# Layer B's attention: TensorE kept in source order, each group in four steps between the k products of the projection tiles

## The chip, the cores and the metric

The kernel runs on one core of a Trainium2 chip. The metric is the device time of one execution in microseconds (us); lower is better. One profiled execution gives the trace.

## The reference, cut to what matters

The model is a decoder trunk of two layers, run for 1024 prompt tokens and 8 decode samples together (1032 columns). The change touches only the second layer, "layer B", and there only the attention. In short:

```python
proj = rms_norm(h) @ w_in_b                      # 768 query columns and 256 memory-query columns
q = rope(proj[..., :768]); cq = proj[..., 768:]
tok_out = swa_attend(q, k, v, sinks)             # 12 heads of 64, window 128, 4 key/value heads, a sink per head
x_out = mem_attend(cq, mem_k, mem_v)             # 4 heads of 64 over 256 memory tokens
h = h + rms_norm(concat(tok_out, x_out) @ w_out) # then the MLP
```

All is float32. Each float32 product is made of three matmuls on rounded halves (high and low part of both operands), so a projection of 1024 inputs has 8 products k = 0 to 7 of three matmuls each.

## The kernel before, in words

The token columns stand in three chunks of 344. A **projection chunk** is one output tile of 128 features over one chunk: `dense_chunk` calls `dense_mm` (L298), which issues 8 products (24 matmuls, L287 to L289) into one PSUM bank of tag `dn`, which has two, and an evacuation by ScalarE follows (L1519).

The **attention** works in 32 groups. A group is one head over 512 tokens: groups 0 to 7 are memory attention, 8 to 31 sliding window. A group has these stages:

- `s1`: 8 score matmuls (L517, L518 or L1602, L1603) into two PSUM banks of tag `ax`, which has four; VectorE reads the maxima (for the window groups it also adds the mask into the tile `Pm`, L1606), ScalarE takes the exponentials (L525 or L1613). The tile `Pm` has tag `p` with four buffers.
- `norm`: VectorE makes the reciprocal of the sums, GpSimd multiplies `Pm` by it in two halves (L431).
- `s2`: 8 transposes of `Pm` on TensorE (L442) into two `ax` banks; each half is rounded by ScalarE and its rest taken by VectorE (`split`, L224) into tiles of tag `t`, which has two buffers, so one group's.
- `s3`: the value matmuls (L460; 4 for a memory group, 10 for a window group) into a bank of tag `ac`, which has two.
- `s4`: ScalarE copies one half (L468), VectorE adds the other, SyncE stores the result to `mixs`.

`run_groups` (L496) calls these one step per group: step i issues `s1` of group i+2, `norm` of i+1, `s3` of i-1, `s2` of i, then the other work that the list `fill` holds for this step, then `s4` of i-1. `fill` holds the 18 chunks of the six query tiles at steps -2, -1, 0, then 4 to 6, 8 to 10, 12 to 14, 16 to 18 and 19 to 21; the three chunks of the second key tile at 7, 11 and 15; rotary embedding and splitting of the queries and keys (`rope`, whose half rotation goes through a transfer, L1526); attention of the samples (`mem_sample` at 8 to 18, `swa_sample` at 26 to 30); and from step 23 on parts of the output projection: 8 chunks `early` of 5 products, 4 chunks `rest` of 3, one `full` of 8. Steps 1 to 3 and 22 hold no projection chunk.

The order of this source is not the order on the engines. When the kernel is built, a scheduler that simulates the engines chooses each engine's order: source order is only the priority, and an instruction whose operands the simulation takes as not ready is overtaken by a later one that is. The order so chosen is fixed in the program. The wrapper `InOrder` (L41) can tie an instruction behind the one traced before it on its engine; before the change it is used for VectorE in part of the MLP alone:

```python
return tc.keep_in_program_order(r) if ordered[0] else r
```

After `run_groups` come the rest of the output projection (`full`, `rest`), the norms and the MLP.

Of the kernel before, what the change touches and what calls it, by code (L numbers as in the profile page):

```python
# [10 lines left out]
F32R = mybir.dt.float32r  # L11
# [5 lines left out]
P = 128  # L17
D = 1024
KT = D // P
# [15 lines left out]
def trunk_kernel(ctx, tc, xT, memT, wia, wib, wkk, wkv, wmk, wo, wu, wd, cmk, cmv, sth, ssk, ssv,  # L35
                 gains, sinkb, sinkc, cosd, sind, identd, lvmd, swmd,
                 yT, mko, mvo, hpo, kpo, vpo, hso, kso, vso):
    nc = tc.nc
    ordered = [False]

    class InOrder:  # L41


        def __init__(self, eng):
            self.eng = eng

        def __getattr__(self, name):
            f = getattr(self.eng, name)

            def call(*args, **kw):  # L50
                r = f(*args, **kw)  # L51
                return tc.keep_in_program_order(r) if ordered[0] else r
            return call

    V, A, T, G, S = nc.vector, nc.scalar, nc.tensor, nc.gpsimd, nc.sync
    V = InOrder(V)
    uid = [0]

    def nm(s):
# [13 lines left out]
    def slot(tag, shape=(P, N), dt=F32):  # L73
        return spool.tile(list(shape), dt, tag=tag, name=nm(tag), bufs=BUFS[tag])
# [211 lines left out]
    def mm3(ps, wh, wl, xh, xl, first, last, more=False):  # L286
        T.matmul(ps, wh, xl, start=first, stop=False, skip_group_check=more)  # L287
        T.matmul(ps, wl, xh, start=False, stop=False, skip_group_check=more)  # L288
        T.matmul(ps, wh, xh, start=False, stop=last, skip_group_check=more)  # L289

    wide, turn_ = [False], [0]

    def dense_bank():
# [4 lines left out]
    def dense_mm(w, c, ks=range(KT), bank=None):  # L298
        ps = (psum(bank) if bank else dense_bank())[:, :CH]
        ks = list(ks)  # L300
        for i, k in enumerate(ks):
            mm3(ps, w[0][:, k * P:(k + 1) * P], w[1][:, k * P:(k + 1) * P], X[:, k, 0, cs(c)], X[:, k, 1, cs(c)],
                i == 0, i == len(ks) - 1)
        return ps

    def dense_chunk(w, c, evac, ks=range(KT)):
# [98 lines left out]
    class Group:  # L405
# [6 lines left out]

        def s1(self):
            self.Pm, self.den = slot("p", (P, 4, 256)), slot("sm", (P, 4))
            self.sink = self.s1f(self.Pm, self.den)

        def norm(self):
            if self.sink is not None:
# [12 lines left out]
                    tt(G, o, o,  # L431
                       self.den[:, j].unsqueeze(2).to_broadcast([P, o.shape[1], o.shape[2]]), ALU.mult)

        def s2(self):
            self.PT = hi, lo = [slot("t", (P, 2 * 512), F32R) for _ in range(2)]
            for hf in range(2):
                ps = psum("ax")
                blocks = [(2 * hf + i // 2, i % 2) if self.window else (i, hf) for i in range(4)]
                i0 = 1 if self.first and hf == 0 else 0
                for i, (j, kb) in enumerate(blocks):  # L440
                    if i >= i0:
                        T.transpose(ps[:, i * P:(i + 1) * P], self.Pm[:, j, kb * P:(kb + 1) * P], ident)  # L442
                sl = slice(hf * 512 + i0 * P, hf * 512 + 512)
                split(ps[:, i0 * P:], hi[:, sl], lo[:, sl], V)

        def s3(self):
            av = self.av = psum("ac")
# [24 lines left out]
    AHEAD = 2  # L472

    def group_steps(gs):

        n = len(gs)

        def do(stage, i):
            if 0 <= i < n:
                getattr(gs[i], stage)()  # L480

        def step(i):
            do("s1", i + AHEAD)
            do("norm", i + 1)
            do("s3", i - 1)
            do("s2", i)
            yield
            do("s4", i - 1)

        out = []  # L490
        for i in range(-AHEAD, n + 1):
            g = step(i)
            out += [lambda g=g: next(g, None)] * 2
        return out

    def run_groups(gs, fill):  # L496
        for i, f in enumerate(group_steps(gs)):
            f()
            if i % 2 == 0:
                for f in fill.get(i // 2 - AHEAD, ()):  # L500
                    f()

    def mem_groups(p, qs, k2, mv, r8):
        gs = []
        for hf in range(2):
            for e in range(2):
                h = 2 * p + e

                def s1(Pm, den, hf=hf, e=e, h=h):
                    mx = slot("sm", (P, 4))  # L510
                    for qq in range(2):
                        ps = psum("ax")
                        for u in range(2):
                            i = hf * 4 + qq * 2 + u
                            o = ps[:, u * 256:(u + 1) * 256]
                            ql = qs[e][:, i * P:(i + 1) * P]
                            T.matmul(o, ql, k2[0][:, h], start=True, stop=False)  # L517
                            T.matmul(o, ql, k2[1][:, h], start=False, stop=True)  # L518
                        m2 = mx[:, 2 * qq:2 * qq + 2]
                        V.reduce_max(m2, ps.rearrange("p (u k) -> p u k", u=2), axis=AX.X)  # L520
                        i0 = hf * 4 + qq * 2
                        V.scalar_tensor_tensor(m2, m2, -1.0, r8[:, i0:i0 + 2], op0=ALU.mult, op1=ALU.mult)
                        for u in range(2):
                            j = 2 * qq + u
                            A.activation(Pm[:, j], ps[:, u * 256:(u + 1) * 256], AF.Exp, bias=mx[:, j:j + 1],  # L525
                                         scale=r8[:, i0 + u:i0 + u + 1], accum_out=den[:, j:j + 1])
                gs.append(Group(e, s1, lambda kb, h=h: mv[:, kb, h * P:(h + 1) * P],
                                lambda ro, src, hf=hf: S.dma_start(mixs[6 + p][ro, hf * 512:(hf + 1) * 512], src)))
        return gs
# [519 lines left out]
    def mlp(l, hsrc, hdst, nxt, Yp):  # L1049
# [394 lines left out]
            weight_load(n)  # L1444
        for n in range(SPLIT, len(ust)):
            hidden_load(n)
        ordered[0] = True
        for n in range(SPLIT):
            hidden_split(n)
            weight_split(n)  # L1450
# [2 lines left out]
        for n, (p, cc, (g, m)) in enumerate(units):  # L1453
            if n + LOAD < len(units):
                weight_load(n + LOAD)
            if n + STAGE < len(units):
                hidden_load(n + STAGE)
            if n + SPLIT < len(units):
                hidden_split(n + SPLIT)
            if n + SPLIT < len(units):  # L1460
                weight_split(n + SPLIT)
            w = split_at.pop(n)
            for c in cc:
                if g == 0:
# [12 lines left out]
            if p == 4 and g == 1:  # L1477
                squares(0, 0, m, cc[0], G)
            if (g, m) == (3, 3):
                if p == 3:  # L1480
                    bg.append(lambda: None)
                    norm(1, 1)
                    norm(1, 0)
                if p == 4:
                    if cc[0] == 0:
                        bg.extend([lambda: None] * 2)
                    norm(0, cc[0])
            elif p in (2, 4):
                tick(1.6 if p == 2 else 1)
            if n + SPLIT >= half:  # L1490
                ordered[0] = False


    def swa_values(wv, vt, kvn, c, r1):
# [87 lines left out]
    def swa_groups(p, qs, ks, vt, swm):  # L1582
        j = p // 3
        gs = []
        for hf in range(2):
            for e in range(2):
# [3 lines left out]
                def s1(Pm, den, hf=hf, e=e, hh=hh):  # L1590
                    kh, kl = ks[e]
                    mx, es = slot("sm", (P, 4)), slot("sm", (P, 4))
                    for qq in range(2):
                        bank = psum("ax")
                        todo = []
                        for jj in (2 * qq, 2 * qq + 1):
# [18 lines left out]
                    return es  # L1615

                def vsrc(t, hf=hf, kvh=kvh):
                    blk = 4 * hf + t - 1
# [272 lines left out]
    def at(i, f, *args):  # L1891
        fill.setdefault(i, []).append(lambda: f(*args))
    load, put, weight, early, rest, full, norm, YB = out_b(hs[1], hs[2])
    parts = ((21, 0, (6, 7, 0)), (22, 0, (1, 2)), (23, 1, (6, 7, 0)), (24, 1, (1, 2)), (25, 0, (3,)), (25, 1, (3,)),
             (27, 2, (6, 7, 0)), (28, 2, (1, 2)), (29, 2, (3,)))
# [13 lines left out]
        at(i, weight, m, (tag, tag))  # L1909
    for p in range(6):  # L1910
        for c in range(NCH):
            at(start[p] + c - (0 if p else AHEAD), q[p][c])
    for c in range(NCH):
        at((7, 11, 15)[c], k1_step, c)
    for i, f in enumerate(mem_sample(1, cqs)):
        at(8 + i, f)
    for i, fs in zip((26, 27, 28, 28, 29, 30, 30), swa_sample(qss, knew)):
        for f in fs:
            at(i, f)
    for i, f, m, c in ((23, early, 0, 0), (24, early, 1, 0), (25, early, 2, 0), (26, early, 0, 1), (27, early, 1, 1), (28, early, 2, 1), (29, early, 3, 0), (30, early, 3, 1), (29, rest, 0, 0), (30, rest, 1, 0), (30, rest, 2, 0), (31, rest, 3, 0), (32, full, 4, 0)):  # L1920
        at(i, f, m, c)
    for i, *h in parts:
        at(i, load, *h)
    run_groups(groups, fill)
    weight(6, ("c", "c"))
    weight(7, ("r", "r"))
    for c in range(NCH):
# [109 lines left out]
```

## Time and profile before

| | |
|---|---|
| three runs | 2542.4, 2543.6, 2545.7 us; median 2543.6 |
| the profiled execution's own time | 2528.8 us |
| its span, first to last instruction | 2526.9 us |
| TensorE busy | 2337.0 us, 92% |
| VectorE, ScalarE, GpSimd busy | 67%, 44%, 56% |
| mean granted TensorE clock | 0.971 of 2.4 GHz |

The profiled execution was 14.8 us shorter than the median run; its span and what lies around it make its own time. Times in the trace count from the first instruction. The attention that the change touches lies between 1436 and 1733 us, in slices 23 to 28 of the 40 of the profile's page.

### The profile page before, as it was taken

The numbers are of one execution on the slowest core, as the hardware profiler recorded it, in microseconds if no ns is written. First come the engines' busy times: TensorE is split into PE (matmuls) and PEld (weight loads), VectorE is DVE, ScalarE is ACT, GpSimd is POOL, SyncE is SP. The second block draws the span as 40 slices with busy tenths as digits, with TensorE's granted clock in tenths as the row PEclk, the third lists the DMA queues.
The fourth block names the chain that finished last, engine by engine and source line by source line (L and its number), as shares of the span: only waits on it lengthen the run. The fifth ranks groups of instructions, "written<-read, shape, count | busy, mean of one in ns | idle before, by whom it ended". The sixth has DMA issues, their size and how long they took to land. (4 is left out here: it accounts for less than half of the span.)

```text
span 2526.9 us, 45370 instructions
## 1 busy us (share of the span) xinstructions
PE 2337.0 (92%) x17055; PEld 2258.4 (89%) x17055; DVE 1693.0 (67%) x2813; ACT 1105.7 (44%) x2457; POOL 1423.9 (56%) x1130
## 2 busy tenths in 40 slices
PE   7998999989899999999999998888999999999997
PEld 6887989989799989999998897777999899999996
DVE  7778677775766665677667367765576665667847
ACT  6573434444433232444354364664443333344424
POOL 4546454453676564657775344544576556557846
PEclk9999999999999999999999998999999999999998
DMA  4335555432345555755663333333335545855482
GB/s 160 134 109 177 164 179 168 161 95 84 113 138 165 167 183 175 246 162 149 197 214 112 106 105 97 108 111 132 120 113 167 171 156 171 277 148 152 127 279 74
DMA packets 231735, 383.00 MB, mean 152 GB/s; under 512 B 27914, under 2 KB 118602, under 8 KB 231500
## 3 DMA queue, kind: packets, MB, share of 16 engines
q1 hardware_dynamic: 154332, 253.80, 30.1%
q10 hardware_dynamic: 77184, 126.31, 17.1%
q8 instruction: 134, 2.20, 0.4%
q14 instruction: 85, 0.70, 0.1%
HBM read 253.27 MB, written 123.56 MB: 149 GB/s over the span
## 5 line engine op out<-in xcount | busy, mean ns | idle before, releaser
L287 PE MATMUL dn<-X,ws 128*128 128x344 f32 (+2 forms) x1136 | 374.0, 330 | 30.8 <-DVE X L51 17.7
L288 PE MATMUL dn<-X,ws 128*128 128x344 f32 (+2 forms) x1136 | 369.0, 325 | 0.0
L289 PE MATMUL dn<-X,ws 128*128 128x344 f32 (+2 forms) x1136 | 368.2, 324 | 0.0
L98 POOL TENSOR_TENSOR ws<-wr,ws 128x512 fp32r<-128x512 f32 (+1 forms) x118 | 222.4, 1887 | 172.3 <-ACT ws L225 161.9
L287 PEld LDWEIGHTS dn<-X,ws 128*128 128x128 f32 x1136 | 219.2, 193 | 41.7 <-DVE X L51 20.2
L51 DVE TENSOR_TENSOR X<-ws,X 128x516 fp32r<-128x516 f32 x160 | 179.6, 1127 | 107.0 <-ACT X L225 106.4
L288 PEld LDWEIGHTS dn<-X,ws 128*128 128x128 f32 x1136 | 219.6, 193 | 1.9 <-issue 0.8
L289 PEld LDWEIGHTS dn<-X,ws 128*128 128x128 f32 x1136 | 219.4, 193 | 1.2 <-issue 0.4
L288 PE MATMUL ax<-X 128*128 128x258 f32 x736 | 209.5, 285 | 2.2 <-POOL X L98 2.2
L287 PE MATMUL ax<-X 128*128 128x258 f32 x736 | 207.8, 284 | 3.0 <-ACT X L225 3.0
L289 PE MATMUL ax<-X 128*128 128x258 f32 x736 | 209.1, 285 | 0.0
L225 ACT CAST ws<-wr 128x1024 fp32r<-128x1024 f32 (+1 forms) x138 | 116.1, 843 | 148.1 <-DMA wfd<-ws 35.5
L98 POOL TENSOR_TENSOR p<-p,sm 128x512 f32<-128x512 f32 (+2 forms) x92 | 87.5, 974 | 127.3 <-DVE sm L51 66.7
L225 ACT CAST X<-ws 128x516 fp32r<-128x516 f32 (+1 forms) x192 | 110.1, 621 | 101.1 <-PE ax L289 48.3
L287 PE MATMUL ax<-X,ws 128*128 128x344 f32 (+2 forms) x472 | 148.0, 315 | 3.1 <-DVE X L51 2.7
L289 PE MATMUL ax<-X,ws 128*128 128x344 f32 (+2 forms) x472 | 145.8, 309 | 0.0
L288 PE MATMUL ax<-X,ws 128*128 128x344 f32 (+2 forms) x472 | 145.5, 308 | 0.0
L287 PE MATMUL ac<-X 128*128 128x258 f32 x496 | 140.2, 284 | 4.6 <-ACT k L1231 3.8
L288 PEld LDWEIGHTS ax<-X 128*128 128x128 f32 x736 | 140.8, 191 | 2.6 <-POOL X L98 2.6
L287 PEld LDWEIGHTS ax<-X 128*128 128x128 f32 x736 | 140.0, 191 | 3.4 <-ACT X L225 3.4
L289 PE MATMUL ac<-X 128*128 128x258 f32 x496 | 140.5, 284 | 0.0
L289 PEld LDWEIGHTS ax<-X 128*128 128x128 f32 x736 | 140.5, 191 | 0.0
(650 smaller groups left out, 8198.3 us busy)
## 6 DMA issues: line engine op xcount, KB each, us to landing
ws<-u ACTq DMA_DIRECT2D x160, 258.0 KB, 2.8
u<-k SPq DMA_DIRECT2D x104, 258.0 KB, 3.9
wr<-wu ACTq DMA_DIRECT2D x104, 256.0 KB, 3.1
wfd<-ws SPq DMA_DIRECT2D x20, 1024.0 KB, 5.0
X<-u21s SPq DMA_DIRECT2D x32, 516.0 KB, 6.3
ct<-u ACTq DMA_DIRECT2D x112, 129.0 KB, 2.7
u<-k SPq DMA_DIRECT2D x104, 129.0 KB, 1.8
u21s<-mv SPq DMA_DIRECT2D x26, 516.0 KB, 3.8
```

The source lines that it names most:

```text
L51: r = f(*args, **kw)
L98: return eng.tensor_tensor(out, a, b, op=op)
L225: A.copy(hi, src)
L287: T.matmul(ps, wh, xl, start=first, stop=False, skip_group_check=more)
L288: T.matmul(ps, wl, xh, start=False, stop=False, skip_group_check=more)
L289: T.matmul(ps, wh, xh, start=False, stop=last, skip_group_check=more)
```

## The change

The wrapper now also covers TensorE, and during `run_groups` every TensorE instruction is tied behind the one traced before it. The stages of a group are cut: `s1` and `s2` each into two halves of one PSUM bank. Step i is now four parts in another order: (1) `s3` of i-1 and the first half of `s2` of i; (2) its second half and `s4` of i-1; (3) the first half of `s1` of i+2 and `norm` of i+1; (4) the second half of `s1` of i+2. Part 1 comes first; the others are called from inside `dense_mm`, between two products k, when a quarter, half and three quarters of the products of that step are out. In a step without projection chunks the four parts follow each other. `fill` has the same entries at the same steps, with the count of their products added. No arithmetic changes.

```diff
-    V, A, T, G, S = nc.vector, nc.scalar, nc.tensor, nc.gpsimd, nc.sync
-    V = InOrder(V)
+    A, G, S = nc.scalar, nc.gpsimd, nc.sync
+    V, T = InOrder(nc.vector, "V"), InOrder(nc.tensor, "T")
...
+    between = []
+
+    def breath():
+
+        if between:
+            between[0]()
...
                 i == 0, i == len(ks) - 1)
+            if i < len(ks) - 1:
+                breath()
         return ps
...
-            self.sink = self.s1f(self.Pm, self.den)
+            self.half = self.s1f(self.Pm, self.den)
+            next(self.half)
+
+        def s1b(self):
+            self.sink = next(self.half)
...
         def step(i):
-            do("s1", i + AHEAD)
-            do("norm", i + 1)
-            do("s3", i - 1)
-            do("s2", i)
+            do(i - 1, "s3")
+            do(i, "s2")
             yield
-            do("s4", i - 1)
+            do(i, "s2b")
+            do(i - 1, "s4")
+            yield
+            do(i + AHEAD, "s1")
+            do(i + 1, "norm")
+            yield
+            do(i + AHEAD, "s1b")
...
     def run_groups(gs, fill):
...
+        steps = group_steps(gs)
+        for i in range(len(steps) // 4):
+            todo, fs = steps[4 * i:4 * i + 4], fill.get(i - AHEAD, ())
+            total, done = sum(k for _, k in fs), [0]
+
+            def due():
+                done[0] += 1
+                while todo and 4 * done[0] >= total * (4 - len(todo)):
+                    todo.pop(0)()
+            between[:] = [due] if total else []
+            todo.pop(0)()
+            for f, k in fs:
+                f()
+                if k:
+                    due()
+            between.clear()
+            while todo:
+                todo.pop(0)()
...
+    ordered.update("T")
     run_groups(groups, fill)
+    ordered.clear()
```

## Rows read from the trace of the kernel before

**Rows 1.** The page: the engines' busy time, and TensorE's granted clock in 40 slices.

```profile
PE 2337.0 (92%) x17055; PEld 2258.4 (89%) x17055; DVE 1693.0 (67%) x2813; ACT 1105.7 (44%) x2457; POOL 1423.9 (56%) x1130
PEclk9999999999999999999999998999999999999998
```

**Rows 2.** Busy us (count) by stretch for PE, PEld, DVE, ACT, POOL; clock; DMA.

```profile
1436.20:1453.50 17.30, 12.51 (x77) 12.05 (x76) 9.94 (x21) 11.23 (x25) 9.41 (x8) 0.84 0.37 125
1453.50:1523.50 70.00, 65.82 (x411) 60.68 (x410) 49.14 (x99) 41.24 (x114) 31.94 (x27) 0.97 0.35 97
1523.50:1657.20 133.70, 118.91 (x734) 103.30 (x734) 99.60 (x262) 78.14 (x224) 58.63 (x53) 0.92 0.34 99
1657.20:1687.10 29.90, 20.13 (x122) 16.57 (x121) 22.66 (x71) 18.16 (x56) 13.65 (x18) 0.89 0.37 113
...
sum 296.90, PE 259.18 PEld 232.10 DVE 207.10 ACT 173.68 POOL 132.02; mean PE 51.84 PEld 46.42 DVE 41.42 ACT 34.74 POOL 26.40
```

**Rows 3.** L287 alone, one matmul per product of a chunk; same columns.

```profile
1523.50:1657.20 133.70, 33.76 (x99) 19.51 (x98) 0.92 0.34 99
...
1436.20:1733.10 296.90, 82.16 (x245) 47.92 (x245) 0.94 0.37 109
```

**Rows 4.** As rows 2: half-clock stretches (first of six, sum), one at full clock.

```profile
1447.89:1454.71 6.82, 4.14 (x17) 3.92 (x18) 2.16 (x9) 6.52 (x20) 2.26 (x3) 0.50 0.00 0
...
sum 37.54, PE 28.72 PEld 27.68 DVE 29.76 ACT 17.57 POOL 16.18; mean PE 4.79 PEld 4.61 DVE 4.96 ACT 2.93 POOL 2.70
...
1635.62:1679.99 44.37, 36.11 (x248) 31.82 (x246) 33.77 (x103) 35.45 (x107) 20.36 (x26) 1.00 0.32 93
```

**Rows 5.** TensorE's waits, 1523.5 to 1657.2: us in total, times, longest.

```profile
PE ax L1602 <- DVE sm L51: 5.0, 4, 2.9
PE ax L1602 <- DVE t L51: 2.7, 2, 2.2
```

**Rows 6.** Timeline, TensorE at full clock; the second row is seven matmuls later.

```profile
1500.05 0.32 PE L287 MATMUL dn<-X,ws 128*128 128x344 f32 x1
...
1501.15 0.32 PE L288 MATMUL dn<-X,ws 128*128 128x344 f32 x1
...
1507.57 0.39 PE L460 MATMUL ac<-t,mv 128*128 128x512 f32 x1
1507.80 0.60 PE L442 MATMUL ax<-ident,p 128*128 128x128 f32 x4
1508.16 0.40 PE L287 MATMUL dn<-X,ws 128*128 128x344 f32 x1
```

**Rows 7.** Timeline of the stage's start, TensorE and GpSimd; in brackets the wait before.

```profile
1450.57 0.58 PE L517 MATMUL ax<-k,q 128*128 128x256 f32 x1 [4.79 <-ACT p L525]
...
1451.96 2.04 POOL L98 TENSOR_TENSOR p<-p,sm 128x512 f32<-128x512 f32 x2 [6.63 <-DVE sm L51]
...
1453.54 1.05 PE L442 MATMUL ax<-ident,p 128*128 128x128 f32 x4
```

**Rows 8.** Timeline: group 25 from its last score matmul to its first transpose.

```profile
1657.05 0.28 PE L1603 MATMUL ax<-k,q 128*128 128x256 f32 x1
...
1658.88 0.35 DVE L51 CUSTOM_DVE_ANT_0 p<-ax,msk,snkb 128x128 f32<-128x128 f32 x1 [0.29 <-DMA mixs<-p]
...
1667.32 0.17 DVE L51 RECIPROCAL sm<-sm 128x4 f32<-128x4 f32 x1
...
1668.20 0.33 PE L442 MATMUL ax<-ident,p 128*128 128x128 f32 x1
```

**Rows 9.** ScalarE's groups, 1453.5 to 1523.5: busy us, mean ns; idle before.

```profile
L525 ACT ACTIVATE p<-ax,sm,r 128x256 f32<-128x256 f32 x26 | 14.4, 564 | 5.8 <-DVE sm L51 3.6 <-DMA mixs<-p 2.1
L225 ACT CAST t<-ax 128x512 fp32r<-128x512 f32 x16 | 9.4, 585 | 3.0 <-DVE sm L51 2.3 <-PE ax L442 0.6
```

**Rows 10.** VectorE's waits, 1436.2 to 1733.1: us in total, times, longest.

```profile
DVE r L51 <- DMA r<-r: 16.6, 6, 4.3
DVE p L51 <- DMA mixs<-p: 11.3, 11, 3.4
```

More of the change, by code (lines that the diff above doesn't have):

```diff
@@ L38, in trunk_kernel, with __init__, __getattr__ @@
     nc = tc.nc
-    ordered = [False]
+    ordered = set()
     class InOrder:
[L44 to L48, printed above, removed]
+        def __init__(self, eng, name):
+            self.eng, self.name = eng, name
+        def __getattr__(self, attr):
+            f = getattr(self.eng, attr)
             def call(*args, **kw):
                 r = f(*args, **kw)
-                return tc.keep_in_program_order(r) if ordered[0] else r
+                return tc.keep_in_program_order(r) if self.name in ordered else r
             return call
-    V, A, T, G, S = nc.vector, nc.scalar, nc.tensor, nc.gpsimd, nc.sync
-    V = InOrder(V)
+    A, G, S = nc.scalar, nc.gpsimd, nc.sync
+    V, T = InOrder(nc.vector, "V"), InOrder(nc.tensor, "T")
     uid = [0]
@@ L432, in norm, with s2 @@
                        self.den[:, j].unsqueeze(2).to_broadcast([P, o.shape[1], o.shape[2]]), ALU.mult)
-        def s2(self):
-            self.PT = hi, lo = [slot("t", (P, 2 * 512), F32R) for _ in range(2)]
-            for hf in range(2):
+        def s2(self, hfs=(0,)):
+            if 0 in hfs:
+                self.PT = [slot("t", (P, 2 * 512), F32R) for _ in range(2)]
+            hi, lo = self.PT
+            for hf in hfs:
                 ps = psum("ax")
@@ L444, in s2, with s2b @@
                 split(ps[:, i0 * P:], hi[:, sl], lo[:, sl], V)
+        def s2b(self):
+            self.s2((1,))
         def s3(self):
@@ L476, in group_steps, with do @@
         n = len(gs)
-        def do(stage, i):
+        def do(i, *stages):
             if 0 <= i < n:
-                getattr(gs[i], stage)()
+                for stage in stages:
+                    getattr(gs[i], stage)()
         def step(i):
-            do("s1", i + AHEAD)
-            do("norm", i + 1)
-            do("s3", i - 1)
-            do("s2", i)
+            do(i - 1, "s3")
+            do(i, "s2")
             yield
-            do("s4", i - 1)
+            do(i, "s2b")
[5 more added lines that the diff above has]
+            do(i + AHEAD, "s1b")
         out = []
@@ L492, in group_steps @@
             g = step(i)
-            out += [lambda g=g: next(g, None)] * 2
+            out += [lambda g=g: next(g, None)] * 4
         return out
     def run_groups(gs, fill):
[L497 to L501, printed above, removed]
+        steps = group_steps(gs)
[15 more added lines that the diff above has]
+                todo.pop(0)()
     def mem_groups(p, qs, k2, mv, r8):
@@ L511, in s1 @@
                     for qq in range(2):
+                        if qq:
+                            yield
                         ps = psum("ax")
@@ L526, in s1 @@
                                          scale=r8[:, i0 + u:i0 + u + 1], accum_out=den[:, j:j + 1])
+                    yield None
                 gs.append(Group(e, s1, lambda kb, h=h: mv[:, kb, h * P:(h + 1) * P],
@@ L1446, in mlp @@
             hidden_load(n)
-        ordered[0] = True
+        ordered.add("V")
         for n in range(SPLIT):
@@ L1490, in mlp @@
             if n + SPLIT >= half:
-                ordered[0] = False
+                ordered.clear()
     def swa_values(wv, vt, kvn, c, r1):
@@ L1593, in s1 @@
                     for qq in range(2):
+                        if qq:
+                            yield
                         bank = psum("ax")
@@ L1614, in s1 @@
                                      accum_out=den[:, jj:jj + 1])
-                    return es
+                    yield es
                 def vsrc(t, hf=hf, kvh=kvh):
@@ L1889, in trunk_kernel, with at @@
     fill = {}
-    def at(i, f, *args):
-        fill.setdefault(i, []).append(lambda: f(*args))
+    def at(i, f, *args, k=0):
+        fill.setdefault(i, []).append((lambda: f(*args), k))
     load, put, weight, early, rest, full, norm, YB = out_b(hs[1], hs[2])
@@ L1911, in trunk_kernel @@
         for c in range(NCH):
-            at(start[p] + c - (0 if p else AHEAD), q[p][c])
+            at(start[p] + c - (0 if p else AHEAD), q[p][c], k=KT)
     for c in range(NCH):
-        at((7, 11, 15)[c], k1_step, c)
+        at((7, 11, 15)[c], k1_step, c, k=KT)
     for i, f in enumerate(mem_sample(1, cqs)):
@@ L1920, in trunk_kernel @@
     for i, f, m, c in ((23, early, 0, 0), (24, early, 1, 0), (25, early, 2, 0), (26, early, 0, 1), (27, early, 1, 1), (28, early, 2, 1), (29, early, 3, 0), (30, early, 3, 1), (29, rest, 0, 0), (30, rest, 1, 0), (30, rest, 2, 0), (31, rest, 3, 0), (32, full, 4, 0)):
-        at(i, f, m, c)
+        at(i, f, m, c, k=5 if f is early else 3 if f is rest else KT)
     for i, *h in parts:
         at(i, load, *h)
+    ordered.update("T")
     run_groups(groups, fill)
+    ordered.clear()
     weight(6, ("c", "c"))
```

## Prediction

> **What bounds the kernel now.** I read the page first. TensorE is busy 92% of the span and no other engine above 67%, so the kernel is bounded by TensorE, by its waits and by its clock [rows 1]. The granted clock in 40 slices is near full, with its dips in a few places. Then the busy time by stretch of the stage that the change touches, 1436.2 to 1733.1 us, the end of the last group's value matmuls. Of 296.9 us TensorE works 259.2 and waits 37.7, which is the most that better order alone could win [rows 2]. The waits are unevenly spread: 4.2 us in the 70 us of the memory groups, 14.8 us in the 133.7 us of the window groups that still have projection chunks, 9.8 us in the 29.9 us of those that have none left [rows 2]. That last stretch is there because the scheduler pulled chunks forward into every early gap: between 1657 and 1687 almost no chunk matmul runs.
>
> The next view is the clock. Six stretches of the stage, 37.5 us together, ran at half clock, 1.2 instead of 2.4 GHz; the first began while TensorE was idle [rows 4]. TensorE was busy for 28.7 us of them, so half of that, 14.4 us, was lost to the clock. Waits and clock together are 52.1 us; the rest is work.
>
> VectorE is busy 99.6 of 133.7 us with the window groups, some 15 of them: 6.6 us a group [rows 2]. It is the second engine, not the bound.
>
> **The change part by part.** No instruction is added or removed; all costs lie in order.
>
> *The work that stays.* The stage before issued 245 products of three chunk matmuls [rows 3]. `run_groups` has 228 (21 chunks of 8, 8 of 5, 4 of 3, one of 8), so 17 belong to what follows it. Chunk matmuls at full clock follow each other at (1501.15 - 1500.05) / 7 = 0.157 us [rows 6], so these are 17 x 3 x 0.157 = 8.0 us, and the same work took 296.9 - 8.0 = 288.9 us. At full clock it is 259.2 - 14.4 - 8.0 = 236.8 us of TensorE. Switching between chunk, transpose and value matmuls is in this sum; the new order switches about as often (four times a step), so I keep it.
>
> *The start.* Group 0's transposes can't run before its probabilities are scaled. GpSimd's first half of that ended at 1451.96 + 1.02 = 1453.0 us; TensorE began the transposes at 1453.54 [rows 7]. What sets this is VectorE, ScalarE and GpSimd, whose instructions the change leaves. TensorE now has in front of them two query chunks (48 x 0.157 = 7.5 us) and 16 score matmuls (1.9 us, estimated at 0.12 each for 256 columns from the 0.157 for 344), and no longer the scores of group 2. It is done at 1436.2 + 9.4 = 1445.6 and waits 7.4 us where it waited 4.8 [rows 7]. The half clock that follows costs the same: 4.14 busy at half clock, 2.1 us [rows 4].
>
> *Steps 1 to 3 have no chunks.* TensorE has some 2.7 us a step: 4 value matmuls of 0.23, 8 transposes at 0.36 for four [rows 6] and 8 scores of 0.12, with a little for switching. In source order the value matmuls of group i wait for ScalarE's cast and VectorE's rest of the transposes, one score product earlier. ScalarE has, for each memory group, four exponentials at 0.56, two casts at 0.59 [rows 9] and a copy of about the same: 4.0 us. I take 4.2 us a step and so 1.5 us of wait, 4.5 for three. Before, chunks stood here and hid this. The bound above is the pace of the window groups without chunks, about 5.4 of them in 29.9 us [rows 2]: 5.5 us, 2.8 of wait each. Below, nothing is hidden for free: ScalarE's 4.0 us alone leave 1.3.
>
> *Step 22* has none either: 5.5 us at that pace, with 20.13 / 5.4 = 3.7 of work of which about 1 is the sample's; I take 2.6 us of wait.
>
> *The other 28 steps* (4 to 21, 23 to 32) each carry 9 to 33 chunk matmuls, spread between transposes and scores. This is the term that decides. Before, the waits per group were 4.2 / 8 = 0.5 us among the memory groups, 14.8 / 15 = 1.0 among the window groups with chunks, 9.8 / 5.4 = 1.8 without [rows 2]. Of the 14.8, 7.7 are scores that waited for a PSUM bank which VectorE had not yet read [rows 5]; in the new order a step uses the four banks in turn, so a bank comes back a whole step (some 8 us) after its matmuls, and these should go. That leaves 0.5. But transposes now stand at fixed places, and anything late at the head of VectorE's queue stops them and all chunks behind. The chain is measured: from group 25's last score matmul to its first transpose 1668.20 - 1657.33 = 10.9 us, though only part of that is work [rows 8]; VectorE stood behind a transfer for the tile `Pm` at its beginning, and the reciprocal waited behind the next group's maxima. The new order gives it two steps, less what lies in a step between its first transposes and its scores: 0.7 of transposes, 18 chunk matmuls or 2.8, 1.0 of scores, 4.5 in all. A window step with 24 chunk matmuls has 3.8 us of those and 4.3 of other work. The latter is from the window stretch: 118.9 busy, less 0.08 x 133.7 x 28.7 / 37.5 = 8.2 lost to the clock, less 99 x 3 x 0.157 = 46.6 for chunks, over 15 groups [rows 2 to 4]. With a wait of 0.7 the step is 8.8, and the chain has 2 x 8.8 - 4.5 = 13.1 us. So it fits, with 2.2 us to spare. The rotation of a query tile holds VectorE for 2.8 us on average and 4.3 at most, six times in the stage, and the next use of a `p` buffer up to 3.4 [rows 10]; these would exceed the spare. I take 0.7 us, between 0.5 and 1.0 and nearer the former because the bank waits go: 28 x 0.7 = 19.6 us. For the range: 0.3, if what remains is hidden too, to 1.8, the rate without chunks.
>
> *The clock.* Before, half clock came after the long waits; in the 44 us from 1635.6 to 1680 TensorE was busy 36.1 us, with many gaps about 1 us long, at clock 1.00 [rows 4]. With waits spread as above I expect the start's 2.1 us and one more stretch of its like, 5 us in all against 14.4.
>
> [...]
>
> *What moves on other queues.* `s4` now comes in the second quarter of a step, so SyncE's store of a group starts earlier and frees its `p` buffer earlier; VectorE's 11.3 us behind such stores [rows 10] are what this eases, at nothing. The weight loads stay at their steps and three weight tiles run ahead; loads into reused `q`, `c` and `r` tiles near the end are in the 0.7 per step.
>
> *Sum.* Waits: 7.4 + 4.5 + 2.6 + 19.6 = 34.1. Total 236.8 + 5.0 + 34.1 = 275.9 us against 288.9: 13.0 us less. After the stage TensorE goes on with the output projection and the MLP as before, so all of it reaches the end. The profiled execution had 2528.8 us and becomes 2515.8; the median of the runs, 2543.6, was 14.8 above, so the forecast for runs is 2543.6 - 13.0 = 2530.6 us.
>
> **The rivals.**
>
> *Waits move, the total stays.* VectorE's blocked moments are the same as before, each stops TensorE as before, and the clock dips with them: 1.0 us in 28 steps (+8.4) and 10 us lost to the clock instead of 5. Result +0.4: 2544 us. For it: VectorE's waits are on transfers and ScalarE [rows 10], which no order of TensorE removes. Against it: half of TensorE's waits there were for banks [rows 5]. The pin may also do little, if matmuls traced after `run_groups`, which are not tied, slip in between; it ends in the same place.
>
> *Slower: the chain doesn't fit.* Each step waits for group i's scaled probabilities, as in the stretch without chunks, since no chunk may overtake a transpose. At 1.8 us in 28 steps, +30.8, the result is 2561 us. It turns from gain to loss at 0.7 + 13.0 / 28 = 1.16 us a step. For it: the chain of 10.9 us against 13.1, and VectorE busy 6.6 of 8.8 us a group; if the step is shorter than I think, the room shrinks by twice that. Against it: 10.9 us was measured with VectorE blocked in it.
>
> *Larger gain.* 0.3 us a step and only the start's half clock: 11.2 + 2.9 more, 2516 us.
>
> [...]
>
> **How the numbers follow.** The forecast case 0.48; the larger gain 0.11; the total stays 0.13; the clock falls 0.04; slower by the chain 0.24. No change is within 0.2%, 5 us, about what a measurement of this kernel can tell. Faster: 0.48 + 0.11 and a part of the rest, 0.60; same 0.16; slower 0.24. The range that should hold the time 8 times in 10 goes from the larger gain, 2515, to 0.7 + 22.5 / 28 = 1.5 us a step, 2553, where about half of the slower case is still inside. The forecast case alone, 0.5 to 1.0 us a step, is 2525 to 2539.
>
> **What would show it.** In the changed profile: TensorE's wait before the first transposes some 7 us; chunk matmuls in groups of about 6 between four transposes and four scores until the end of the stage, and no stretch like 1657 to 1687 but step 22; fewer and shorter half-clock stretches; no score product that waits for VectorE longer than a microsecond; the last value matmuls about 15 to 20 us earlier, with 17 products fewer in front of them. It would be wrong if transposes wait for GpSimd or VectorE in most steps (then the chain is too long), if the stage shrinks but the waits after it grow by the same, or if VectorE, now in a new order of its own, is blocked longer.

## The result and the profile after

The changed kernel takes 2563.9 us (median of four runs, 2562.1 to 2565.5), the kernel before 2543.3 us on the same chip: a ratio of 1.0079, 95% interval 1.0062 to 1.0097. It is 20.6 us slower where 13.0 us less was forecast, and it lies above the range. The profiled execution took 2563.0 us.

The first profile of before was 14.8 us under its median. A second one, made for the experiments, took 2536.8 us where the median on its chip was 2537.8. The 11 us between its stage's start and the first one's arose ahead of the stage, 8.6 of them before 1309 us; the stage itself was the same, 297.0 against 296.9 us, with a wait of 36.8 against 37.7. I compare traces with the second one.

The page of the changed kernel first: TensorE's busy time and its granted clock in 40 slices, as in [rows 1].

```profile
PE 2349.1 (92%) x17055; PEld 2275.4 (89%) x17055; DVE 1695.8 (66%) x2813; ACT 1114.8 (44%) x2460; POOL 1419.6 (55%) x1130
PEclk9999999999899999999999989889999999999998
```

The same instructions, and TensorE is busy 12 us longer. Between 1400 and 1800 us the clock dips in slices 24, 26 and 27. Then the stage by stretch, columns as in [rows 2]: the whole from the first score to the last value matmul, and by phase.

```profile
1447.50:1759.20 311.70, 251.97 (x1543) 229.34 (x1542) 206.06 (x529) 174.24 (x480) 125.90 (x120) 0.89 0.34 102
...
1445.70:1462.80 17.10, 9.81 (x65) 9.24 (x64) 10.49 (x20) 9.70 (x18) 8.94 (x8) 0.95 0.36 126
1470.90:1495.30 24.40, 14.36 (x66) 10.72 (x65) 18.82 (x34) 13.96 (x35) 9.32 (x8) 0.72 0.29 81
1495.30:1526.80 31.50, 31.50 (x216) 30.50 (x214) 18.92 (x46) 18.45 (x53) 12.36 (x12) 1.00 0.25 68
1526.80:1672.40 145.60, 119.89 (x713) 106.81 (x712) 95.45 (x250) 75.99 (x210) 55.02 (x53) 0.87 0.34 98
1672.40:1681.30 8.90, 5.63 (x39) 5.09 (x38) 5.61 (x20) 6.42 (x22) 2.82 (x3) 0.91 0.65 193
1681.30:1759.20 77.90, 64.50 (x424) 60.76 (x423) 54.02 (x157) 46.60 (x130) 35.19 (x36) 0.92 0.40 124
```

TensorE waits 311.70 - 251.97 = 59.7 us in the stage. By phase, length less busy: the start 7.3, steps 1 to 3 10.0, steps 4 to 7 nothing at all, steps 8 to 21 25.7, step 22 3.3, steps 23 to 32 13.4. Next the half-clock stretches as in [rows 4], the first and the last of ten.

```profile
1461.17:1467.99 6.82, 5.17 (x20) 5.11 (x21) 3.87 (x8) 3.91 (x13) 4.08 (x4) 0.50 0.01 2
...
1727.41:1734.23 6.82, 6.10 (x25) 6.07 (x26) 3.25 (x10) 0.96 (x2) 1.27 (x2) 0.50 0.26 77
sum 71.66, PE 54.54 PEld 51.56 DVE 48.96 ACT 32.18 POOL 27.77; mean PE 5.45 PEld 5.16 DVE 4.90 ACT 3.22 POOL 2.78
```

Half of the 54.54 us, 27.3, I count as lost to the clock, against 16.1 in the second profile of before (32.1 busy in 41.0). Half is my estimate from the granted 0.50. In the first profile of before, in its stretch at half clock from 1570.77, one chunk matmul starts at 1575.62 and the seventeenth after it at 1580.49, all in a row: 0.286 us each. That is 1.82 times the 0.157 of [rows 6], so by the chunk matmuls 45% of the busy time would be nearer, 24.6 us against 14.5; the sums below keep half, as the prediction did. At 344 columns a matmul that is 1.20 columns a ns, and 2.19 at full clock. The 1.2 and 2.4 GHz of the prediction come out of the first and the granted 0.50 as an estimate, with a column counted as a cycle.

The waits of TensorE over the stage, as in [rows 5]:

```profile
PE ac L51 <- DVE t L51: 23.0, 11, 6.1
PE ax L51 <- DVE ct L51: 11.6, 4, 5.7
PE ax L51 <- POOL p L98: 10.8, 4, 6.6
PE ac L51 <- ACT t L225: 6.7, 4, 3.3
```

No score product waits for a bank that VectorE has not read, as predicted; one, in step 3, waits 1.9 us for a bank that ScalarE's exponentials (L565) read. Scaled probabilities (`p` from GpSimd) are late four times, 6.6 of the 10.8 us at the start. The time goes to value matmuls that wait for VectorE's rest `t`, and to transposes that wait for a tile `ct`: those are the samples' softmax.

Against the second profile of before the balance closes. Waits: 59.7 - 36.8 = 22.9 more. Clock: 27.3 - 16.1 = 11.2 more. Work at full clock: 252.0 - 27.3 = 224.7, and 83 chunk matmuls fewer than before lie in the stage (650 against 733 in the traces), at 0.157 us 13.0 us of work that now lies outside it: 12 matmuls, 1.9 us, stand in front of the first score (from 1445.64 us), the others behind the stage; 237.7 against 260.2 - 16.1 = 244.1 is 6.4 less. The sum is 27.7 us more; the stage is 14.7 longer and 13.0 of its work lies outside it. The two profiled executions are 26.2 us apart, the medians on one chip 20.6.

### The profile page after: what moved, and what is told of

It is laid out like the page before. It is cut to its first block, busy times and chain, and to the rows that moved or that the text cites. A ratio compares the mean times of both kernels' runs of the same rounds, so it can differ in the third digit from the quotient of the medians.

```text
span 2561.2 us, 45354 instructions
## 1 busy us (share of the span) xinstructions
PE 2349.1 (92%) x17055; PEld 2275.4 (89%) x17055; DVE 1695.8 (66%) x2813; ACT 1114.8 (44%) x2460; POOL 1419.6 (55%) x1130
## 5 line engine op out<-in xcount | busy, mean ns | idle before, releaser
L51 PE MATMUL dn<-X,ws 128*128 128x344 f32 (+2 forms) x3408 | 616.9, 330 | 31.9 <-DVE X L51 17.7
L51 PEld LDWEIGHTS dn<-X,ws 128*128 128x128 f32 x3408 | 550.7, 196 | 43.0 <-DVE X L51 20.4
L51 PE MATMUL ax<-X 128*128 128x258 f32 x2208 | 278.9, 285 | 5.3 <-ACT X L225 3.0
L51 PEld LDWEIGHTS ax<-X 128*128 128x128 f32 x2208 | 272.2, 191 | 6.3 <-ACT X L225 3.5
L51 PE MATMUL ax<-X,ws 128*128 128x344 f32 (+2 forms) x1416 | 223.4, 313 | 2.9 <-DVE X L51 2.7
L51 PEld LDWEIGHTS ax<-X,ws 128*128 128x128 f32 x1416 | 211.2, 195 | 5.5 <-DVE X L51 3.8
L51 PEld LDWEIGHTS ac<-X 128*128 128x128 f32 x1488 | 183.0, 189 | 4.1 <-ACT k L1272 3.3
L51 PE MATMUL dn<-X 128*128 128x258 f32 x960 | 123.3, 283 | 4.6 <-DVE X L51 3.2
L51 PEld LDWEIGHTS dn<-X 128*128 128x128 f32 x960 | 118.1, 189 | 5.9 <-DVE X L51 3.6
L98 POOL TENSOR_TENSOR X<-p,X 128x512 fp32r<-128x512 f32 (+1 forms) x56 | 85.9, 1549 | 25.1 <-ACT X L225 21.8
L51 DVE SCALAR_TENSOR_TENSOR k<-k 128x258 f32<-128x258 f32 x156 | 91.8, 600 | 3.0
```

Of the source, the lines that this page charges most:

```text
L98: return eng.tensor_tensor(out, a, b, op=op)
```

## The experiments

All ratios are to the kernel before on the same chip, with 95% intervals. "The stage" is always from the first score to the last value matmul.

**The kernel before, once more.** Its use is told above.

> The kernel before, unchanged, profiled once more. Its first profiled execution was 14.7 us shorter than the median of its runs, while the changed kernel's was within 1 us of its own. If that execution was a lucky one, this profile gives 2540 to 2546 us and shows in which stage the 15 us came; the stage of layer B's attention then lies within 5 us of the first profile's 296.9. If profiling shortens this kernel, it gives about 2529 again.

Measured: 2536.8 us, neither of the two values expected, and 1.0 us under the median on its chip; the stage is the same as in the first profile, as expected of it.

**The order without the tie.** The four parts of a step and their places stay; only the tie goes.

```diff
-    ordered.update("T")
     run_groups(groups, fill)
```

> The changed kernel without the tie of TensorE: the new order of the four parts and the calls between the products stay as priorities, the scheduler may let matmuls overtake. If the tie is the cost (theory: in source order a group's value matmuls and transposes stand behind VectorE's late work and hold all chunks behind them), this runs at 2538 to 2550 us, as before the change. If the new order of the stages is the cost, in layer A's attention too, it runs at 2558 to 2566 us.

Measured: 2528.5 us, 0.9956 (0.9938 to 0.9974). Its stage and its waits:

```profile
1452.70:1733.10 280.40, 246.24 (x1591) 224.94 (x1590) 201.86 (x529) 173.81 (x484) 126.68 (x121) 0.95 0.38 114
```

```profile
PE ac L51 <- DVE t L51: 5.5, 6, 2.6
PE ax L51 <- POOL p L98: 4.4, 2, 2.2
```

The waits for `t` are 5.5 us instead of 23.0 and there is none for `ct`. TensorE waits 34.2 us in all and loses 13.1 to the clock (26.2 busy at half clock). The time lies below both expected ranges. The order that was costed as a gain is one; what it was tied with is not.

**The tie without the new order.** The kernel before, with the wrapper of the change and TensorE tied during `run_groups`.

```diff
+    ordered.update("T")
     run_groups(groups, fill)
+    ordered.clear()
```

> The kernel before with TensorE tied to source order during layer B's groups, nothing else: chunks stay whole between a group's transposes and its last stage. If the tie is the cost, 2560 us or more; since here no chunk stands between transposes and score products, the spread over four parts would be worth something and this is slower than the changed kernel, 2565 to 2585. If the new order is the cost, 2540 to 2550.

Measured: 2550.3 us, 1.0039 (1.0013 to 1.0066).

```profile
PE ac L51 <- DVE t L51: 26.5, 19, 4.9
PE ax L51 <- DVE ct L51: 10.2, 4, 6.1
```

The same two sorts of wait, of the same size, stand in the old order once it is tied: the tie makes them. But it costs 0.39% there (0.13 to 0.66) and 1.0079 / 0.9956 = 1.0124 on the new order, three times as much by these medians. I had expected 2565 to 2585 us, more than the changed kernel takes; by the medians the tied old order is the faster of the two tied ones. In the profiled stages the tie adds 21.8 us of waits and clock to the old order (74.7 against 52.9) and 39.7 to the new one (87.0 against 47.3); on the old order work at full clock gives 5.6 us of that back, on the new one 0.8.

**The samples' transposes a step later.** The softmax of the samples and its transposes are two entries of `fill` instead of one, for both sample attentions.

```diff
+        def turn():
+            pm, pz = box["pm"], box["pz"]
+            ps = psum("ax")
+            for kb in range(2):
                 T.transpose(ps[:, kb * 32:(kb + 1) * 32], pm[:, kb * P:(kb + 1) * P], ident[:32, :32])
...
-        return ([start] + [lambda b=b: score(b) for b in range(4)] + [softmax]
+        return ([start] + [lambda b=b: score(b) for b in range(4)] + [softmax, turn]
```

> The changed kernel with the samples' softmax cut before its transposes, which are issued one step later (memory sample: its values and its end also one step later). In the changed profile TensorE waits 5.0 + 0.4 us and 5.7 us at these transposes, and runs 6.8 us at half clock after each. If these waits are lost time of their own, 11 us of waits and 3 to 5 us of clock go: 2564 - 15 = 2549 us, range 2545 to 2554. If VectorE is simply behind and the wait moves to the next value matmuls, 2558 to 2566.

Measured: 2549.1 us, 1.0051 (1.0035 to 1.0067).

```profile
PE ac L51 <- DVE t L51: 24.3, 16, 6.8
...
PE ax L51 <- DVE s L51: 6.1, 1, 6.1
...
PE ax L51 <- DVE ct L51: 1.4, 2, 0.9
```

The wait for the softmax falls from 11.6 to 1.4 us. A new one of 6.1 appears behind the transposes of the samples' result (`s`), which the edit shifted too; in the changed kernel it was 1.0. The waits for `t` stay. Of the first theory's 11 us of waits a part came back in other places: TensorE's waits fell by 7.6 us. By the ratio its 2545 to 2554 us, which were given for a kernel before of 2543.3, are missed at 2556.

**VectorE tied as well.**

```diff
-    ordered.update("T")
+    ordered.update("TV")
```

> VectorE's instructions of layer B's attention are tied to source order as TensorE's are; all else is the changed kernel (1.0079). Theory 1, the waits come from the order that the scheduler gave to VectorE: then each group's rest of the transposes comes before work that is traced behind it, the waits of the value matmuls for t (23.0 us in the changed kernel) fall to under 10, and the time to about 0.999. Theory 2, the waits come from what VectorE itself waits for, the transfer of a rotated query tile above all: in source order the rope product stands as near to its transfer as before or nearer, and VectorE has no choice left of what to do instead: the t waits stay at 20 or more, and the time is 1.008 or up to 1.02. I hold 2 for likelier (0.6).

Measured: 2600.4 us, 1.0257 (1.0221 to 1.0293), more than either theory said. VectorE's largest wait in sum, and TensorE's:

```profile
DVE t L51 <- ACT t L225: 101.0, 43, 4.2
```

```profile
PE ac L51 <- DVE t L51: 29.6, 13, 5.5
PE ax L51 <- POOL p L98: 25.0, 22, 2.4
```

In source order the rest of `t` stands right behind ScalarE's cast, and VectorE now stands there 101 us (11.2 in the changed kernel). So source order is worse for VectorE than the scheduler's order. That doesn't clear the scheduler's: an order with the rest of `t` ahead of the rope work was not tried. GpSimd's probabilities become late in 22 places here: this is what the rival of the chain looks like when it is true.

**The query tiles' rotations a step later.** The tie on TensorE stays; `late` is set for the query tiles.

```diff
-            tt(V, raw[:, sl], raw[:, sl], cosb[:, sl], ALU.mult)
+            r = tt(V, raw[:, sl], raw[:, sl], cosb[:, sl], ALU.mult)
+            if late:
+                tc.keep_in_program_order(r)
...
-            at(start[p] + j - (0 if p else 1), q[p][j])
+            at(start[p] + j + (1 if p else 0), q[p][j])
```

> A query tile's rotation and split are taken one step later than in the changed kernel (tied, so that the scheduler does not pull the product forward on VectorE); the samples stay where they are. Theory 2, the transfer at the head of VectorE's queue makes the t waits: they fall from 23.0 us to about 8, the waits for ScalarE's t with them, and some 5 us of clock: 1.0079 - 17/2543 = about 1.001 (0.998 to 1.004). Theory 1, VectorE is simply too late by its load and order: the waits move to other products, 1.007 to 1.010.

Measured: 2546.9 us, 1.0037 (1.0021 to 1.0053). VectorE's wait behind the rotation's transfer falls from 14.4 us (7 times) to one of 3.2, and TensorE's waits are:

```profile
DVE r L51 <- DMA r<-r: 3.2, 1, 3.2
...
PE ac L51 <- DVE t L51: 20.4, 14, 5.6
PE ax L51 <- POOL p L98: 14.1, 9, 6.6
...
PE ac L51 <- ACT t L225: 1.7, 3, 1.0
```

The time is within the range of the theory at its upper end, but the waits for `t` fell by 2.6 us and not by 15: half a miss. What went are the waits for ScalarE's `t` (5.0 us less) and one for VectorE's `p` (3.1); those for GpSimd's `p` grew by 3.3. In all TensorE waits 9.7 us less in the stage, and the clock's loss is 7.8 less (19.5). The longest of those left, 5.64 us, is behind the one transfer that is left; here are VectorE and TensorE in that place, in brackets the wait:

```profile
1659.80 2.37 DVE L51 TENSOR_TENSOR r<-r,c 128x512 f32<-128x512 f32 x2 [3.17 <-DMA r<-r]
1662.09 0.68 DVE L51 TENSOR_TENSOR t<-ax,t 128x512 fp32r<-128x512 f32 x1
...
1662.82 1.44 PE L51 MATMUL ac<-t,wr 128*128 128x256 f32 x5 [5.64 <-DVE t L51]
```

**Both later, and the samples' result too.** The two edits together, with the copy and the transposes of the samples' result in two steps as well.

```diff
+        def copy():
+            avs = box["avs"] = chunk_tile(256)[:32]
             V.tensor_copy(avs, box["av"][:32, :256])
+
+        def out():
+            avs = box["avs"]
             ps = psum("ax")
```

> Query rotations a step later, the samples' transposes behind their softmax a step later, and the transposes of the samples' values a step later too; TensorE tied. Theory, the tie costs time only where something late stands right in front of the tied instruction: gains of the two single edits add (the samples alone 14 us, the rotations alone 17 if theory 2 holds), plus some 5 for the values' transposes: 1.0079 - 36/2543 = 0.994, near the order without the tie (0.9956). Rival, the tie costs in any place, since there is always something late: not under 1.001.

Measured: 2535.8 us, 0.9990 (0.9976 to 1.0005): 23 us less than the change, but between the theory and its rival.

```profile
PE ac L51 <- DVE t L51: 17.6, 15, 3.0
PE ax L51 <- POOL p L98: 13.4, 7, 6.6
PE ax L51 <- DVE s L51: 5.1, 1, 5.1
```

No wait for `t` is over 3.0 us any more. TensorE still waits 41.7 us (286.10 less 244.40 busy).

**Layer A's groups in their old order,** the tie off. `group_steps` serves layer A's memory groups too, so the change reorders them as well, without a tie.

```diff
-    weave(group_steps(mem_groups(0, qsA, k2, mv, r8) + mem_groups(1, cq1[0], k2, mv, r8)),
+    weave(group_steps(mem_groups(0, qsA, k2, mv, r8) + mem_groups(1, cq1[0], k2, mv, r8), True),
```

> The new order without the tie (0.9956), but layer A's memory groups get back their old order of two parts. If all of the gain is from layer B's stage, as its trace shows (13.5 us shorter there): 0.9956 again, 0.994 to 0.9975. If layer A's order has a share of the gain: 0.998 or above; if it cost something: under 0.994.

Measured: 2527.4 us, 0.9955 (0.9941 to 0.9968). Layer A's order has no share.

**The chunk matmuls free.** Transposes, scores, values and samples stay tied to each other, the three matmuls of a chunk product don't.

```diff
     def mm3(ps, wh, wl, xh, xl, first, last, more=False):
-        T.matmul(ps, wh, xl, start=first, stop=False, skip_group_check=more)
+        nc.tensor.matmul(ps, wh, xl, start=first, stop=False, skip_group_check=more)
...
```

> The changed kernel (1.0079), but the three matmuls of a chunk product are not tied; transposes, scores, value matmuls and the samples' products keep the source order among themselves. Theory, the tie costs because the chunk matmuls may not pass a late transpose or value matmul: with them free the waits are filled again, and nearly all of the distance to the order without the tie (0.9956) comes back: 0.996 to 1.000, with waits of the value matmuls for t under 10 us. Rival, the cost lies in the tied attention products standing behind one another (a sample's late transpose in front of the groups' products): then chunks run dry behind them and 1.003 to 1.008 stays.

Measured: 2550.1 us, 1.0038 (1.0021 to 1.0054). The waits for `t` are 6.2 us, as the theory said, but the time is the rival's. The freed chunks run ahead until no bank is left; one place, 9.3 us:

```profile
1573.44 0.69 DVE L51 TENSOR_TENSOR r<-r,c 128x512 f32<-128x512 f32 x1 [3.05 <-DMA r<-r]
1574.16 1.64 DVE L51 TENSOR_TENSOR q<-r,q 64x512 fp32r<-64x512 f32 x1
1575.81 1.68 DVE L51 TENSOR_TENSOR r<-r,c 128x520 f32<-128x520 f32 x1
...
1578.24 0.17 DVE L51 TENSOR_SCALAR sm<-sm 128x4 f32<-128x4 f32 x1
...
1578.44 0.30 ACT L1653 ACTIVATE sm<-sm,snkb 128x4 f32<-128x4 f32 x1 [9.55 <-DVE sm L51]
...
1582.19 0.81 ACT L1560 COPY r<-dn 128x344 f32<-128x344 f32 x2
...
1582.70 0.66 PE L287 MATMUL dn<-X,ws 128*128 128x344 f32 x1 [9.27 <-ACT r L1560]
```

VectorE stands behind the rotation's transfer, then does the product and the split, some 4.8 us, ahead of a scaling of 0.17 us; ScalarE's exponentials wait for that scaling, and behind them in ScalarE's queue stands the copy that empties the chunk's bank. It is the same blocked moment, reaching TensorE by another way.

**The later places without the tie.** The kernel of "both later", less TensorE's tie; the rope products stay tied on VectorE.

> The later rotations and samples (0.999 with the tie) without the tie. If the scheduler, where it is free, already put other work in front of the late products, the edits bring nothing there: 0.9956 as for the order alone, 0.994 to 0.9975. If the late work also cost time without the tie: under 0.993. If the later places crowd the steps behind them: above 0.998.

Measured: 2516.1 us, 0.9910 (0.9889 to 0.9931), the fastest version. My likeliest value, no gain over the order alone, was wrong. TensorE waits 29.9 us:

```profile
1446.20:1717.80 271.60, 241.75 (x1572) 217.13 (x1571) 197.75 (x529) 173.54 (x482) 123.49 (x121) 0.96 0.38 118
```

**The later rotations alone, without the tie.** The edit of the rotations, on the order without the tie.

> The new order without the tie (0.9956), with the query tiles' rotations one step later and tied on VectorE, the samples where the change has them. With the samples later too it was 0.991. If the rotation's transfer at the head of VectorE's queue is what that gained: 0.991 to 0.993 here as well. If the samples' later transposes gained it: 0.9945 to 0.9965. If each has a share: between.

Measured: 2525.4 us, 0.9954 (0.9935 to 0.9972): nothing over 0.9956. So what 0.9910 has more comes with the samples' edits, alone or together with the rotations: the samples' edits alone were not run without the tie, and the two intervals only just fail to meet (0.9931 and 0.9935).

**The kernel before with a later rotation.** The rope product of five of the six query tiles (the first tile's stays) stands right in front of the sums and the split, which stay where they are; the product of each tile is tied on VectorE.

```diff
-            at(start[p] + j - (0 if p else 1), q[p][j])
+            at(start[p] + (NCH + 1 if p else j - 1), q[p][j])
```

> The kernel before, with one edit alone: the query tiles' rope product a step later (right in front of the sums and the split, which stay) and tied on VectorE. If the transfer at the head of VectorE's queue cost the old order too, as VectorE's 16.6 us behind it say: 0.994 to 0.998. If the old order hides it, since half of its waits were scores that waited for a bank: 0.999 to 1.001. If the product now delays the split and the scores behind it: above 1.001.

Measured: 2530.1 us, 0.9960 (0.9943 to 0.9977). VectorE's wait behind the transfer, 16.6 us in [rows 10], is gone but for one:

```profile
DVE r L51 <- DMA r<-r: 1.9, 1, 1.9
```

The old order had paid for the transfer at VectorE's head too, and one moved product wins there what the whole new order wins. TensorE's waits in the stage fell by 3.2 us (33.6 against 36.8) and the clock's loss by 3.2 (12.9).

## Why the prediction was wrong, step by step

Its own sum, beside what the changed kernel's trace gives:

| term | predicted | measured | from |
|---|---|---|---|
| work at full clock | 236.8 | 230.0 | 252.0 - 27.3, and the 34 of 684 chunk matmuls outside the stage, 12 in front of the first score and 22 at its end, x 0.157 |
| start | 7.4 | 7.3 | stretch from 1445.7 |
| steps 1 to 3 | 4.5 | 10.0 | stretch from 1470.9 |
| step 22 | 2.6 | 3.3 | stretch from 1672.4 |
| 28 other steps | 19.6 | 39.1 | the three other stretches |
| clock | 5.0 | 27.3 | half of 54.54 |
| sum | 275.9 | 317.0 | |

**The step that failed** is the one that "decides": 28 steps at 0.7 us. They took 39.1 / 28 = 1.4 us, past the 1.16 where the sum turned from gain to loss. I had read the waits of before as a rate per step, and priced the tie by taking the bank waits out of that rate. But that rate was one of a free TensorE, which put chunks in front of whatever was late; tied, it could not. The waits also don't come as a rate: steps 4 to 7 have none, at 6.5 us a step (in two of them the second four transposes start at 1496.68 and 1503.21 in the timeline), and most of the rest is lumps of 3 to 6 us. I named the mechanism in the prediction, that anything late at the head of VectorE's queue would stop the transposes and all chunks behind, and that the rotation "would exceed the spare", and then left its price in the 0.7. One lump in the changed kernel, VectorE, ScalarE, TensorE and SyncE's issue:

```profile
1639.57 1.86 SPq L1567 DMA_DIRECT2D r<-r  x3
...
1642.71 0.59 ACT L225 CAST t<-ax 128x512 fp32r<-128x512 f32 x1
...
1646.22 2.37 DVE L51 TENSOR_TENSOR r<-r,c 128x512 f32<-128x512 f32 x2 [3.44 <-DMA r<-r]
...
1648.51 1.59 DVE L51 TENSOR_TENSOR X<-ct,X 128x344 fp32r<-128x344 f32 x1
...
1650.30 0.68 DVE L51 TENSOR_TENSOR t<-ax,t 128x512 fp32r<-128x512 f32 x1
...
1651.03 1.86 PE L51 MATMUL ac<-t,wr 128*128 128x256 f32 x7 [4.99 <-DVE t L51]
```

The cast was done at 1643.3, and the rest of `t`, 0.68 us of work, could have followed. VectorE stood on the rope product, whose transfer was issued from 1639.57, and took `t` up at 1650.30, 7.0 us late: 2.9 us behind the transfer, the others behind the product itself and other work. For those 2.9 us VectorE was idle and still did not take `t` ahead of the product.

The product doesn't need what the transfer brings. It overwrites `raw` in place (`tt(V, raw, raw, cosb)`), and the transfer, which fills `rot`, still reads `raw`; the rotated half is used by GpSimd's product and by the later sum. By the source a product into another tile would not have to wait. No run tries that.

The longest lump, in step 3, shows that the transfer's wait is not all of it. It makes most of the 10.0 us of steps 1 to 3:

```profile
1478.89 1.07 ACT L225 CAST t<-ax 128x512 fp32r<-128x512 f32 x2
...
1479.43 2.37 DVE L51 TENSOR_TENSOR r<-r,c 128x512 f32<-128x512 f32 x2 [2.88 <-DMA r<-r]
...
1485.34 0.69 DVE L51 TENSOR_TENSOR t<-ax,t 128x512 fp32r<-128x512 f32 x1
...
1486.09 1.99 PE L51 MATMUL ac<-t,mv 128*128 128x512 f32 x3 [6.06 <-DVE t L51]
```

VectorE's wait for the transfer ended while ScalarE made the casts. The 5.9 us from there to `t` are VectorE's product, the sum of the rotation and other work that the scheduler had put ahead.

**Overlooked.** The tie covers everything that `fill` traces, the samples' products too. Their softmax and its transposes are one entry, so TensorE reaches the transposes while the softmax is still being made. In the changed kernel, from the maximum to the transposes and the value matmuls that had been ready behind them:

```profile
1579.60 0.41 DVE L51 TENSOR_REDUCE sm<-ac 32x1 f32<-32x256 f32 x1
...
1581.89 0.45 ACT L607 ACTIVATE ct<-ac,sm 32x256 f32<-32x256 f32 x1
...
1583.98 0.23 PE L51 MATMUL ax<-ident,ct 32*128 32x32 f32 x1 [4.96 <-DVE ct L51]
...
1584.80 1.11 PE L51 MATMUL ac<-t,c 128*128 128x256 f32 x4
```

No term of the sum held these 11.6 us. That `group_steps` also orders layer A was overlooked too, and costs nothing.

**The clock** is the second term that failed, and the larger miss: 27.3 us and not 5.0. I had expected half clock after the start and once more; there are ten stretches, and each of the nine longest waits runs into one or has one begin within 1.2 us behind it. So every lump was paid about one and a half times: the waits grew by 22.9 us over before and the clock's loss by 11.2.

**What held.** The start's wait (7.3 against 7.4), partly by luck: the first score comes 1.9 us later than I had it, behind four products of the first chunk, and from there to the first transpose it took 15.3 us and not the 17.3 of before; no score waits for VectorE to read a bank; no stretch without chunks but steps 1 to 3 and 22. The work came out 6.8 us lower than I had kept, and about as low in the versions without the tie and with the tie alone (both 238.5 us with the chunk matmuls outside the stage added, as in the balance above, against 244.1 before and 237.7).

**The rivals.** "The chain doesn't fit" gave 2561 us and the result is 2563.9, but its mechanism is not what happened: by it each step waits for GpSimd's probabilities, and past the start that is 4.2 us in three places. The chain had the room that I gave it; what was late were short pieces of VectorE's work that are not in the chain. "Waits move, the total stays" had the right cause, VectorE's blocked moments stopping TensorE as before, with too small a price. "The clock falls", at 0.04, was meant of the steps without chunk matmuls and did not show: steps 1 and 2 have none and ran at a granted 1.00 (1470.90 to 1481.65 us); it fell to 0.50 at 1481.65, inside step 3's wait of 6.1 us. What transposes alone do to the clock no run shows.

**What the experiments show.** The tie makes the loss and the order makes a gain: 0.9956 without the tie, 1.0039 with it alone. That the two kinds of late work carry a large part of the tie's price is shown by moving them: 1.0051, 1.0037, and 0.9990 with all of it. That they carry all of it is refuted: the same placement without the tie is at 0.9910, so a tied TensorE still costs 0.8%, 20 us. In the two profiled stages that is 11.8 us of waits (41.7 against 29.9; those for `t` are 17.6 against 2.4, those for GpSimd's `p` 13.4 against 2.6) and 10.2 us of the clock's loss (19.5 against 9.3). Freeing only the chunks doesn't repair it. The gains were as much the clock's as the waits': against the changed kernel the samples' edit took 7.6 us of waits and 8.5 of the clock's loss, the rotations' 9.7 and 7.8, all of it 18.0 and 7.8. Open is why the tie costs more on the new order than on the old, how much of the clock's loss belongs to which wait, and how much of the lateness of `t` is the transfer's and how much the order of VectorE's other work: with the transfer's waits down from 14.4 to 3.2 us the waits for `t` still were 20.4.

## What to carry to other kernels

Here a tie in source order was to be priced by what is late at each tied place, not by the average wait of the free order: that average was what was left after the scheduler had covered what was late. Before tying an engine, list each instruction that will stand in it right behind its producer, the side streams' too, and look on the producer's engine for an instruction that waits for a transfer at the head of its queue, also one that only overwrites what the transfer reads. The cheap repair is to move that instruction: one rope product, moved a step, won 0.4% on the old order, though nothing on the new order without the tie (0.9954 against 0.9956).

## What was not expected

Two profiled executions of the same kernel before differ by 8.0 us (2528.8 and 2536.8), and all of it, and 3 us more, arose ahead of the stage that was studied; inside it they agree within 0.2 us. An offset of the stage's start between two traces says nothing about a change inside it.

The tie on VectorE cost more than any other edit, 1.0257, though VectorE is busy only 210 of the 353 us of its stage: the order of an engine that is not the bound decided over the time of the one that is.
